# Scores of the prompt from float16 pairs instead of float32r pairs in a two-layer streaming encoder

## The chip, the cores and the metric

The kernel runs on one core of a Trainium2 chip. The core has a matrix engine (TensorE, "PE" in the profile, with its weight loads shown as "PEld"), a vector engine (VectorE, DVE), an activation engine (ScalarE, ACT), a general engine (GpSimd, POOL) and a queue engine (SyncE, SP) from which this kernel issues all its DMA transfers. The metric is the device time of one execution in microseconds (us), as the median of several runs.

## The reference

Two attention layers follow each other, for a prompt of 2048 tokens and, beside it, a sample of 64 new tokens with a cache. Of each layer the shape is this:

```python
def gated_attention_layer(x_p, x_s, ck, cv, norm_g, w_in, q_g, k_g, w_out, ...):
    qp, kp, vp, gp = project(x_p, norm_g, w_in, q_g, k_g, n_heads, n_kv)
    op = prompt_band_attention(qp, kp, vp, past_chunks, bias_fn, sinks)
    y_p = x_p + (op * jax.nn.silu(gp)) @ w_out
    ...                       # the same for the sample, with the cache before its keys

def project(x, norm_g, w_in, q_g, k_g, n_heads, n_kv):
    p = rms_norm(x, norm_g) @ w_in
    ...                       # split in q, k, v, gate
    q = rms_norm(q.reshape(..., HEAD_DIM), q_g)
    k = rms_norm(k.reshape(..., HEAD_DIM), k_g)

def attend(q, k, v, bias, valid, sinks):
    s = einsum('bqkgd,bskd->bkgqs', qg, k) * (dh ** -0.5) + bias
    ...                       # softmax over the keys, in layer A with a learned sink
    o = einsum('bkgqs,bskd->bqkgd', p, v)
```

The model is 1024 wide and a head has 64 dimensions. Layer A has 16 query heads on 2 key heads and looks at its own chunk of 64 tokens and 2 chunks before it; layer B has 16 query and 16 key heads and looks 8 chunks back. All is in float32.

## The kernel before

**Two parts for one number.** To reach nearly float32 with operands of fewer bits, the kernel writes a factor as a sum of a high and a low part. In the projections of layer A both parts are float32r, in those of layer B float16. For the scores before the change, both parts are float32r in both layers.

**How a score is made.** A head has 64 dimensions and a tile 128 partitions, so the high and the low part of the keys lie one above the other: `KA` and `KB` (one for each of two key heads) have 128 partitions, 64 with the high part and 64 with the low part, and one column for each token. The queries come as two stationary matrices: `q1` holds the high part of the query in both halves, `q2` the low part in the half that meets the high part of the keys, and zeros in the other half. Two matmuls that add up in PSUM then give (q high)(k high + k low) + (q low)(k high). The queries are loaded as weights; the keys are the moving operand.

**Who makes the parts.** A transposed tile of queries or keys lies in PSUM. ACT writes the high part with a scale for each dimension (`qsc` is minus the query's norm weight, `ksc` is 8 times the key's; the signs are turned since the kernel works with the negative score). DVE then computes the scaled value minus the high part (lines L1043, L1082, L1343, L1347). The second copy of the high part of the queries, in the other 64 partitions, is made by a DMA from the tile to itself (L1090 in layer A, L1336 in layer B).

**Layer A** (from L1037 on) goes through 4 groups of 4 query heads and, in each, through 17 tiles: 16 of 128 prompt tokens and the sample of 64. A tile has one group of 8 score matmuls (L1121 for `q1`, L1122 for `q2`, for 4 heads) over up to 256 keys. The queries of a tile are made two tiles ahead of their scores.

**Layer B** (from L1307 on) goes through 8 pairs of heads and, in each, through 8 units of 256 prompt tokens and the sample. A unit has 4 groups of score matmuls, one for each half unit and head (L1392 for `q1`, L1393 for `q2`). A half unit looks at up to 640 keys, which the program takes in two pieces: 384 and 256 keys from the fifth tile on, less before. The 640 scores go through DVE (L1396, adds the bias and takes the minimum), ACT (L1400, the exponential), back through PE (L830, transposes), ACT and DVE again (L805, L806, the two parts of the probabilities) and PE (L1487, the product with the values).

**What sets the order.** PE's order is written out by the program: a "filler" hands out the matmuls of the projections and of the output projections, piece by piece, by a running count of their estimated cost, and the attention steps stand between. On ACT, DVE, POOL and SP a scheduler orders the instructions by its own estimate of time. The filler's counts hold no term for the scores.

**The sample** uses the same code, with `KSA`, `KSB` (float32r) as its keys. In layer A its `q1` and `q2` come from the same buffers as the prompt's; in layer B it has a tile `QS` of its own, whose unused blocks are zeros.

Of the kernel before, what the change touches and what calls it, by code (L numbers as in the profile page):

```python
# [55 lines left out]
def hybrid_encoder_kernel(  # L56
# [68 lines left out]
    qsc = const([P, 2], "qsc")  # L125
    ksc = const([P, 2], "ksc")
    kgr = const([P, 2, 2 * HD], "kgr")
    sink = const([P, 16], "sink")
# [4 lines left out]
    def constants():  # L133
        load(qkg, qk_gain)
        load(sink, sinks.partition_broadcast(P))
        load(tab[:32], t5_table)
        held["oh"] = oh = t("row", [P, VL], 2)
        load(oh[:32, :VL], t5_onehot)
        load(kgr, k_gain_row.partition_broadcast(P))
        nc.vector.tensor_scalar(qsc, qkg[:, 0:2], -1.0, 1.0, op0=ALU.mult, op1=ALU.mult)  # L140
        nc.vector.tensor_scalar(ksc, qkg[:, 2:4], HD ** 0.5, 1.0, op0=ALU.mult, op1=ALU.mult)
        nc.vector.tensor_scalar(nsink, sink, -1.0, 1.0, op0=ALU.mult, op1=ALU.mult)
        nc.vector.tensor_scalar(kgr, kgr, HD ** 0.5, 1.0, op0=ALU.mult, op1=ALU.mult)
# [753 lines left out]
    def layer_a():  # L897
# [131 lines left out]
        def keys(it):  # L1029
# [4 lines left out]
            transpose(tp, it.kv[:n, 0:128])  # L1034
            gk = ksc[:, 0:1]
            if it.unit[0] == NU:
# [5 lines left out]
            for kk, rows in zip(kd, halves):  # L1042
                nc.vector.scalar_tensor_tensor(  # L1043
                    kk[64:128], tp[rows], gk[rows], kk[0:64].bitcast(F32),
                    op0=ALU.mult, op1=ALU.subtract,
                )
# [20 lines left out]
        def queries(it, tp):  # L1067
            n = it.tile[2]
            it.q1 = q1 = t("q1", [P, 4, P], 2, F32R)
            it.q2 = q2 = low_queries().rearrange("p (h s) -> p h s", h=4)  # L1070
            d1 = [q1.rearrange("p (j e) s -> p j e s", e=2)[:, :, hh, :n] for hh in range(2)]
            d2 = [q2.rearrange("p (j e) s -> p j e s", e=2)[0:64, :, hh, :n] for hh in range(2)]
            src = [tp[r].rearrange("p (j s) -> p j s", j=2) for r in halves]
            for hh, rows in enumerate(halves):
                nc.scalar.activation(d1[hh][rows], src[hh], AF.Identity, scale=qsc[rows, 0:1])
            it.todo = []
            it.low = d1, d2, src

        def lows(it):
            d1, d2, src = it.low  # L1080
            for hh, rows in enumerate(halves):
                nc.vector.scalar_tensor_tensor(  # L1082
                    d2[hh], src[hh], qsc[rows, 0:1], d1[hh][rows].bitcast(F32),
                    op0=ALU.mult, op1=ALU.subtract,
                )
            for hh, rows in enumerate(halves):
                if it in items[-3:]:
                    nc.scalar.activation(d1[hh][halves[1 - hh]], src[hh], AF.Identity, scale=qsc[rows, 0:1])
                else:
                    load(d1[hh][halves[1 - hh]].bitcast(F32), d1[hh][rows].bitcast(F32))  # L1090

# [146 lines left out]
    def layer_b():  # L1238
# [69 lines left out]
        def queries(it):  # L1308
            for q in it.todo:
                bg.run(q)  # L1310
            u, T, tiles = it.unit
            gk = ksc[:, 1:2]
            if u == 1:
# [16 lines left out]
            for hh, rows in enumerate(halves):  # L1330
                nc.scalar.activation(q1[hh][rows], qt[hh], AF.Identity, scale=qsc[rows, 1:2])
# [9 lines left out]
            def low(hh, rows):  # L1341
                def fn():
                    nc.vector.scalar_tensor_tensor(  # L1343
                        q2[hh][rows], qt[hh], qsc[rows, 1:2], q1[hh][rows].bitcast(F32),
                        op0=ALU.mult, op1=ALU.subtract,
                    )
                    nc.vector.scalar_tensor_tensor(  # L1347
                        kd[hh][halves[1 - hh]], kt[hh], gk[rows], kd[hh][rows].bitcast(F32),
                        op0=ALU.mult, op1=ALU.subtract,
                    )  # L1350
                    if it in its[-2:]:
                        nc.scalar.activation(
                            q1[hh][halves[1 - hh]], qt[hh], AF.Identity, scale=qsc[rows, 1:2]
                        )
# [455 lines left out]
```

## Time and profile before

| | us |
|---|---|
| median of 3 runs | 2246.05 |
| lowest and highest | 2245.26, 2250.43 |
| the profiled execution | 2247.64 |
| its span, from first to last instruction | 2245.9 |

The profiled execution is 1.6 us above the median of the runs, and 1.7 us of its time lie outside its span. Matmuls are pipelined: a matmul's duration in a row runs from its start to the end of its last result, and the next one begins long before that. What a matmul costs in a stream is therefore the distance from its start to the start of the next one. The layers lie in the span as follows: layer A's attention to about 690 us, beside it the projections of layer A; then the output projection of A and the first projections of B; layer B's attention from about 900 to 2087 us; the rest of the output projection of B to the end.

### The profile page before, as it was taken

How to read it: one execution, taken by the hardware profiler on the slowest of the kernel's cores; microseconds unless marked ns; L12 is line 12 of the kernel's file. 1: busy time of each engine (PE TensorE's matmuls, PEld its weight loads, DVE VectorE, ACT ScalarE, POOL GpSimd, SP SyncE). 2: the span in 40 equal slices, each digit the busy share in tenths (PEclk: the TensorE clock that was granted, in tenths of full speed). 3: DMA queues.
4: the chain of work that ended last, by engine and by line, in shares of the span. 5: the costliest groups of instructions: out<-in, count | busy, mean ns of one | idle time of the engine just before them, and what ended most of it. 6: DMA issues, size and time to landing. Idle time of an engine off the chain costs nothing.

```text
span 2245.9 us, 41785 instructions
## 1 busy us (share of the span) xinstructions
PE 2175.9 (97%) x13931; PEld 1651.6 (74%) x13931; DVE 1566.4 (70%) x4042; ACT 1421.1 (63%) x3610; POOL 860.2 (38%) x1396
## 2 busy tenths in 40 slices
PE   7999999999999999999999999999999999998999
PEld 6878888788889997556666666666666666566888
DVE  6768777677675456877676776877767767577652
ACT  6878878677785333666676665766666667566430
POOL 5645544334354455753333333333333333232000
PEclk9999999999999999999999999999999999999999
DMA  8857547856545677554243342432434434223664
GB/s 273 272 164 221 185 131 224 234 165 192 181 136 176 213 208 238 183 167 132 90 150 113 100 151 85 151 106 87 155 95 124 130 88 125 79 70 105 195 196 126
DMA packets 254072, 348.96 MB, mean 155 GB/s; under 512 B 29776, under 2 KB 191328, under 8 KB 253824
## 3 DMA queue, kind: packets, MB, share of 16 engines
q1 hardware_dynamic: 253856, 346.29, 50.6%
q8 instruction: 110, 1.80, 0.3%
q14 instruction: 106, 0.87, 0.1%
HBM read 257.59 MB, written 73.43 MB: 147 GB/s over the span
## 4 chain that ended last, share of the span: by engine, by line
PE 69%; DVE 11%; DMA 7%; ACT 7%; issue 3%; POOL 2%; SPq 1%; ACTq 0%; DVEq 0%; POOLq 0%
PE pj L668 12%; PE pj L670 11%; PE pj L669 11%; PE sb L830 4%; PE pj L1653 4%; PE pj L1654 4%; PE pj L1655 4%; PE o L1487 4%; PE tp L830 2%; DMA scan<-in_w_in_b_dram 2%; PE sb L1392 2%; PE sb L1393 2%; PE sa L830 2%; DVE p L1396 1%; DVE pl L806 1%
## 5 line engine op out<-in xcount | busy, mean ns | idle before, releaser
L668 PE MATMUL pj<-wh,xx 128*128 128x512 f16 (+2 forms) x1648 | 639.6, 388 | 4.2 <-ACT pb L691 3.1
L670 PE MATMUL pj<-wh,xx 128*128 128x512 f16 (+2 forms) x1648 | 624.2, 379 | 2.5 <-POOL xx L553 2.5
L669 PE MATMUL pj<-wh,xx 128*128 128x512 f16 x1024 | 389.6, 380 | 0.0
L1400 ACT ACTIVATE p<-p,nm 128x640 f32<-128x640 f32 (+5 forms) x264 | 199.5, 756 | 230.8 <-DVE nm L1396 228.3
L1653 PE MATMUL pj<-xx,wh 128*128 128x264 f32 (+1 forms) x1024 | 289.6, 283 | 5.1 <-DVE res L1663 3.6
L1654 PE MATMUL pj<-xx,wh 128*128 128x264 f32 (+1 forms) x1024 | 286.9, 280 | 0.0
L806 DVE SCALAR_TENSOR_TENSOR pl<-sb,ph 128x640 f16<-128x640 f32 (+4 forms) x256 | 189.0, 739 | 101.5 <-ACT ph L805 98.9
L669 PE MATMUL pj<-wl,xx 128*128 128x512 f32 (+1 forms) x624 | 233.7, 374 | 2.6 <-DVE wl L459 2.6
L553 POOL TENSOR_TENSOR xx<-xraw,xx 128x528 fp32r<-128x528 f32 (+4 forms) x144 | 184.4, 1300 | 86.5 <-ACT xx L552 80.1
L830 PE MATMUL sb<-ident,p 128*128 128x128 f32 x1144 | 206.7, 277 | 4.6 <-DVE pl L806 2.7
L1232 POOL TENSOR_TENSOR o<-gt,o 128x256 f32<-128x256 f32 (+1 forms) x132 | 100.0, 758 | 285.6 <-ACT p L1138 92.4
L1396 DVE CUSTOM_DVE_ANT_0 p<-sb,BT 128x640 f32<-128x640 f32 (+5 forms) x272 | 196.2, 721 | 18.3 <-PE sb L1393 12.8
L745 POOL TENSOR_TENSOR sq<-pa 128x256 f32<-128x256 f32 (+2 forms) x187 | 113.1, 605 | 228.1 <-ACT pa L704 140.8
L750 POOL TENSOR_TENSOR f<-f,mhalf 128x4 f32<-128x4 f32 (+2 forms) x187 | 191.8, 1026 | 14.1
L830 PEld LDWEIGHTS sb<-ident,p 128*128 128x128 f32 x1144 | 149.2, 141 | 62.7 <-DVE pl L806 16.4
L805 ACT ACTIVATE ph<-sb 128x640 f16<-128x640 f32 (+4 forms) x256 | 160.4, 627 | 54.9 <-PE sb L830 53.5
L670 PEld LDWEIGHTS <-xx 128*128 128x128 f16 x1024 | 100.5, 98 | 124.8 <-POOL xx L553 3.0
L1138 ACT ACTIVATE p<-p,nm 128x257 f32<-128x257 f32 (+2 forms) x272 | 134.3, 497 | 49.6 <-DVE nm L1132 43.5
L668 PEld LDWEIGHTS <-xx 128*128 128x128 f16 x1024 | 100.3, 98 | 77.5 <-ACT xx L552 1.4
L669 PEld LDWEIGHTS <-xx 128*128 128x128 f16 x1024 | 101.1, 99 | 67.6 <-issue 1.9
L1487 PE MATMUL o<-pl,values 128*128 128x256 f16 (+1 forms) x672 | 149.4, 255 | 0.0
L1487 PEld LDWEIGHTS <-values 128*128 128x128 f16 x1344 | 134.1, 101 | 15.8 <-issue 0.2
(258 smaller groups left out, 5391.7 us busy)
## 6 DMA issues: line engine op xcount, KB each, us to landing
xx<-xsb SPq DMA_DIRECT2D x112, 512.0 KB, 3.8
xx<-xsa SPq DMA_DIRECT2D x88, 512.0 KB, 5.0
xraw<-oga SPq DMA_DIRECT2D x64, 264.0 KB, 3.8
xraw<-ogb SPq DMA_DIRECT2D x64, 264.0 KB, 3.7
xsa<-xx SPq DMA_DIRECT2D x32, 512.0 KB, 4.3
scan<-in_w_in_b_dram SPq DMA_DIRECT2D x64, 256.0 KB, 4.5
wl<-in_w_in_b_dram SPq DMA_DIRECT2D x64, 256.0 KB, 4.2
q<-q SPq DMA_DIRECT2D x250, 64.0 KB, 2.7
```

The source lines that it names most:

```text
L553: nc.gpsimd.tensor_tensor(lo, rv, wide(hi), op=ALU.subtract)
L668: nc.tensor.matmul(ps[:n, :C], xh, wh, start=k == 0, stop=False)
L669: nc.tensor.matmul(ps[:n, :C], xh, wl, start=False, stop=False)
L670: nc.tensor.matmul(ps[:n, :C], xl, wh, start=False, stop=k == KC - 1)
L750: nc.gpsimd.tensor_tensor(fv, fv, mhalf[:n, :H], op=ALU.pow)
L806: b = nc.vector.scalar_tensor_tensor(dst_lo, src, scale, wide(dst_hi), op0=ALU.mult, op1=ALU.subtract)
L830: nc.tensor.transpose(out, in_, ident[:n, :n])
L1396: mi = nc.vector.tensor_tensor_reduce(out=p[r, :nk], in0=S[r, o : o + nk], in1=b, op0=ALU.add, op1=ALU.min, scale=1.0, scalar=3e38, accum_ ...
L1400: ex = nc.scalar.activation(p[:n, :nk], p[:n, :nk], AF.Exp, scale=-1.0, bias=it.nm[:n, c : c + 1], accum_out=it.sm[:n, c : c + 1],)
L1487: nc.tensor.matmul(it.O[:, h * T + q0 : h * T + q1_], vt, p[:, c, q0:q1_], start=start, stop=stop)
L1653: nc.tensor.matmul(ps[:, :OT], wh, oh, start=k == 0, stop=False)
L1654: nc.tensor.matmul(ps[:, :OT], wh, ol, start=False, stop=False)
```

## The change

`KA`, `KB`, `q1` and `q2` of the prompt become float16 in both layers, half as many bytes. The range of float16 is narrow, so the scales are dealt out anew: of the product of the two norm weights of a dimension, times 8, the key gets a power of two (`kf`: the exponent of the product, divided by 8, held between 1 and 32768) and the query the rest (`qf`, held within plus and minus 60000). The product of the two scales stays what it was. The sample keeps float32r and the old scales; in layer A its queries now lie in `QS`, `q1` in the left half of each block and `q2` in the right, and `QS` is set to zero once more before layer B.

```diff
@@ constants()
+        nc.vector.tensor_tensor(qf, qsc, ksc, op=ALU.mult)
+        nc.vector.tensor_scalar(kf.bitcast(I32), qf.bitcast(I32), 0x7F800000, None, op0=ALU.bitwise_and)
+        nc.vector.tensor_scalar(kf, kf, 0.125, 1.0, op0=ALU.mult, op1=ALU.max)
+        nc.vector.tensor_scalar(kf, kf, 2.0 ** 15, 1.0, op0=ALU.min, op1=ALU.mult)
+        inv = t("ms", [P, 8])[:, 0:2]
+        nc.vector.reciprocal(inv, kf)
+        nc.vector.tensor_tensor(qf, qf, inv, op=ALU.mult)
+        nc.vector.tensor_scalar(qf, qf, 60000.0, -60000.0, op0=ALU.min, op1=ALU.max)
...
-    KA = const([P, SEQ], "KA", F32R)
-    KB = const([P, SEQ], "KB", F32R)
+    KA = const([P, SEQ], "KA", F16)
+    KB = const([P, SEQ], "KB", F16)
...
-    Q2 = [const([P, 512], f"q2_{i}", F32R) for i in range(2)]
+    Q2 = [const([P, 512], f"q2_{i}", F16) for i in range(2)]
@@ layer A, keys()
-            gk = ksc[:, 0:1]
+            gk = (kf, ksc)[it.unit[0] == NU][:, 0:1]
@@ layer A, queries() and lows()
-            it.q1 = q1 = t("q1", [P, 4, P], 2, F32R)
-            it.q2 = q2 = low_queries().rearrange("p (h s) -> p h s", h=4)
+            if it.unit[0] == NU:
+                it.q1, it.q2 = q1, q2 = QS[:, :, 0:TS], QS[:, :, TS:P]
+            else:
+                it.q1 = q1 = t("q1", [P, 4, P], 2, F16)
+                it.q2 = q2 = low_queries().rearrange("p (h s) -> p h s", h=4)
+            gq = (qf, qsc)[it.unit[0] == NU]
...
-                    load(d1[hh][halves[1 - hh]].bitcast(F32), d1[hh][rows].bitcast(F32))
+                    load(wide(d1[hh][halves[1 - hh]]), wide(d1[hh][rows]))
@@ layer B, queries()
-                it.q1 = t("q1", [P, 2, UT], 2, F32R)
+                it.q1 = t("q1", [P, 2, UT], 2, F16)
...
-                    load(q1[hh][halves[1 - hh]].bitcast(F32), q1[hh][rows].bitcast(F32))
+                    load(wide(q1[hh][halves[1 - hh]]), wide(q1[hh][rows]))
@@ layer B, pipeline()
+            zero(QS)
```

The lines below the new ones in `constants()` move down by 10, and those below layer A's `queries` by 14 to 16, so that L1392 before is L1408 after. On PE, in one group of scores of layer B (`sb` the scores in PSUM, `KB` the keys, `q` the two query matrices, `pj` a projection on either side), there stands before:

```order
L670 LDWEIGHTS xx_19815
L670 MATMUL pj_20023<-wh_18509,xx_19815 128x512
L1392 MATMUL sb_20052<-KB,q_3946_19793 128x384
L1393 MATMUL sb_20052<-KB,q_1_109 128x384
L1392 MATMUL sb_20052<-KB,q_3946_19793 128x256
L1393 MATMUL sb_20052<-KB,q_1_109 128x256
L668 LDWEIGHTS xx_19817
L668 MATMUL pj_20023<-wh_18770,xx_19817 128x512
```

and in the same place after:

```order
L680 LDWEIGHTS xx_19822
L680 MATMUL pj_20030<-wh_18516,xx_19822 128x512
L1408 LDWEIGHTS q_3943_19800
L1408 MATMUL sb_20059<-KB,q_3943_19800 128x384
L1409 LDWEIGHTS q_1_111
L1409 MATMUL sb_20059<-KB,q_1_111 128x384
L1408 LDWEIGHTS q_3943_19800
L1408 MATMUL sb_20059<-KB,q_3943_19800 128x256
L1409 LDWEIGHTS q_1_111
L1409 MATMUL sb_20059<-KB,q_1_111 128x256
L678 LDWEIGHTS xx_19824
L678 MATMUL pj_20030<-wh_18777,xx_19824 128x512
```

A float32r matmul loads its weights itself; a float16 one has the load as an instruction of its own. The program has 1472 such loads more, one for each score matmul of the prompt, and PE's order is otherwise as it was.

On DVE, in the first 16 us of the program (`wl` low parts of the first weights, `qsc`, `ksc`, `kgr` constants, `G` and `o` sums of squares), there stands before:

```order
L140 TENSOR_SCALAR qsc<-qkg 128x2
L141 TENSOR_SCALAR ksc<-qkg 128x2
L142 TENSOR_SCALAR nsink<-sink 128x16
L459 TENSOR_SCALAR wl_179<-wraw_129,gain,wh_178 128x256
L143 TENSOR_SCALAR kgr<-kgr 128x256
L459 TENSOR_SCALAR wl_187<-wraw_133,gain,wh_186 128x256 x2
L580 TENSOR_TENSOR o_49_232<-res_230 128x256
```

and after:

```order
L144 TENSOR_TENSOR qf<-qsc,ksc 128x2
L145 TENSOR_SCALAR kf<-qf 128x2
L146 TENSOR_SCALAR kf<-kf 128x2
L153 TENSOR_SCALAR kgr<-kgr 128x256
L469 TENSOR_SCALAR wl_197<-wraw_135,gain,wh_196 128x256
L147 TENSOR_SCALAR kf<-kf 128x2
L469 TENSOR_SCALAR wl_197<-wraw_135,gain,wh_196 128x256
L149 RECIPROCAL ms_162<-kf 128x2
L590 TENSOR_TENSOR o_50_242<-res_240 128x256
L150 TENSOR_TENSOR qf<-qf,ms_162 128x2
```

The seven new instructions (the last of them, L151, stands a little further on) lie between the splits of the first weights.

On POOL, where layer A ends (`p` with the sinks of the sample's last two pairs of heads, `o` an output, `G` a gate, `xx` the output projection's activations), there stands before:

```order
L1145 TENSOR_TENSOR G_8988<-pb_8584,sm_8974 128x256
L1130 COPY p_9105<-nsink 64x2
L1232 TENSOR_TENSOR o_1996_9083<-gt_9057,o_1996_9083 128x256
L1130 COPY p_9111<-nsink 64x2
L553 TENSOR_TENSOR xx_8941<-xraw_8930,xx_8941 128x528
```

and after:

```order
L1159 TENSOR_TENSOR G_8994<-pb_8591,sm_8980 128x256
L1144 COPY p_9111<-nsink 64x2
L849 MEMSET QS 128x512
L1246 TENSOR_TENSOR o_1993_9089<-gt_9063,o_1993_9089 128x256
L1144 COPY p_9117<-nsink 64x2
L563 TENSOR_TENSOR xx_8947<-xraw_8936,xx_8947 128x528
```

The memset of `QS` waits for the sample's last score matmuls of layer A, which read it, and the copy of the second pair's sinks stands behind it. Elsewhere the orders of ACT, DVE, POOL and SP differ by swaps of neighbours; on SP, the load of one bias tile (L317, the third of the second head group) moves back behind two other loads in the first 65 us.

More of the change, by code (lines that the diff above doesn't have):

```diff
@@ L1043, in keys @@
                 nc.vector.scalar_tensor_tensor(
-                    kk[64:128], tp[rows], gk[rows], kk[0:64].bitcast(F32),
+                    kk[64:128], tp[rows], gk[rows], wide(kk[0:64]),
                     op0=ALU.mult, op1=ALU.subtract,
@@ L1311, in queries @@
             u, T, tiles = it.unit
-            gk = ksc[:, 1:2]
+            sample = u == NU
+            gk, gq = ((kf, qf), (ksc, qsc))[sample]
+            gk, gq = gk[:, 1:2], gq[:, 1:2]
             if u == 1:
@@ L1343, in fn @@
                     nc.vector.scalar_tensor_tensor(
-                        q2[hh][rows], qt[hh], qsc[rows, 1:2], q1[hh][rows].bitcast(F32),
+                        q2[hh][rows], qt[hh], gq[rows], wide(q1[hh][rows]),
                         op0=ALU.mult, op1=ALU.subtract,
@@ L1347, in fn @@
                     nc.vector.scalar_tensor_tensor(
-                        kd[hh][halves[1 - hh]], kt[hh], gk[rows], kd[hh][rows].bitcast(F32),
+                        kd[hh][halves[1 - hh]], kt[hh], gk[rows], wide(kd[hh][rows]),
                         op0=ALU.mult, op1=ALU.subtract,
@@ L1352, in fn @@
                         nc.scalar.activation(
-                            q1[hh][halves[1 - hh]], qt[hh], AF.Identity, scale=qsc[rows, 1:2]
+                            q1[hh][halves[1 - hh]], qt[hh], AF.Identity, scale=gq[rows]
                         )
```

14 lines of the change are left out of this document (8 added, 6 removed).

## The prediction

> **What bounds the kernel now.** I read the busy shares first, then the chain that ended last, then busy time by stretch (columns: stretch, its length, busy us of PE, PEld, DVE, ACT, POOL, granted clock, DMA share, GB/s), then PE's waits.
>
> ```profile
> PE 2175.9 (97%) x13931; PEld 1651.6 (74%) x13931; DVE 1566.4 (70%) x4042; ACT 1421.1 (63%) x3610; POOL 860.2 (38%) x1396
> PE 69%; DVE 11%; DMA 7%; ACT 7%; issue 3%; POOL 2%; SPq 1%; ACTq 0%; DVEq 0%; POOLq 0%
> 60.00:700.00 640.00, 628.63 (x3618) 534.47 (x3617) 467.45 (x1451) 493.91 (x1376) 308.89 (x541) 1.00 0.62 189
> 900.00:2090.00 1190.00, 1160.43 (x7279) 770.60 (x7278) 879.11 (x2167) 776.82 (x1956) 416.80 (x716) 1.00 0.39 118
> PE tp L830 <- ACT gt L1219: 7.8, 6, 2.6
> ...
> PE pj L668 <- ACT pb L712: 0.2, 1, 0.2
> ```
>
> PE is busy 98% of both stretches that hold scores (628.63 of 640, 1160.43 of 1190); DVE, the next engine in layer B, 74%. The list of PE's waits, of which the first and the last row stand here (time in all, times, longest), has 24 rows with 59 waits and 64 us. So PE is the bound, and PE time saved should mostly come off the end.
>
> **What a score matmul costs now.** By shape, there are these (the other two of each four of a shape have the same count: L1393 and `KB` in layer B, L1122 and `KB` in layer A):
>
> ```profile
> L1392 PE MATMUL sb<-KA,q 128*128 128x384 f32 x96 | 49.1, 512 | 3.0 <-ACT q L1352 2.9
> L1392 PE MATMUL sb<-KA,q 128*128 128x256 f32 x128 | 39.1, 308 | 0.0
> L1392 PE MATMUL sb<-KA,q 128*128 128x128 f32 x16 | 6.6, 410 | 0.0
> L1121 PE MATMUL sa<-KA,q 128*128 128x256 f32 x120 | 29.7, 280 | 0.0
> L1121 PE MATMUL sa<-KA,q 128*128 128x128 f32 x8 | 2.6, 343 | 4.0 <-ACT res L647 4.0
> ```
>
> The durations overlap, so the price is the distance between starts. Two full groups (384 and 256 keys) of layer B in order of time, with the float16 projection around them (start us, duration):
>
> ```profile
> 1304.73 0.38 PE L669 MATMUL pj<-wh,xx 128*128 128x512 f16 x1
> 1304.94 0.38 PE L670 MATMUL pj<-wh,xx 128*128 128x512 f16 x1
> 1304.97 0.52 PE L1392 MATMUL sb<-KB,q 128*128 128x384 f32 x1
> ...
> 1305.98 0.38 PE L669 MATMUL pj<-wh,xx 128*128 128x512 f16 x1
> ...
> 1309.35 0.38 PE L670 MATMUL pj<-wh,xx 128*128 128x512 f16 x1
> ...
> 1310.38 0.38 PE L669 MATMUL pj<-wh,xx 128*128 128x512 f16 x1
> ```
>
> From L670 to the L669 behind the group pass 1.04 and 1.03 us. In it lie two projection matmuls (L670 and the L668 after the group) at 0.215 each (0.21 to 0.22 between neighbours such as L669 and L670 here). That leaves 0.61 and 0.60 us for the four score matmuls, the change between the two number formats included.
>
> What float16 matmuls of these widths cost, this kernel shows in the products with the values (256 and 128 columns); beside them a float32r score of 128:
>
> ```profile
> 1307.98 0.22 PE L1487 MATMUL o<-pl,values 128*128 128x128 f16 x1
> 1308.04 0.28 PE L830 MATMUL sb<-ident,p 128*128 128x128 f32 x1
> 1308.15 0.27 PE L1487 MATMUL o<-pl,values 128*128 128x256 f16 x1
> ...
> 1308.92 0.38 PE L668 MATMUL pj<-wh,xx 128*128 128x512 f16 x1
> 909.58 0.28 PE L1393 MATMUL sb<-KB,q 128*128 128x128 f32 x1
> 909.70 0.39 PE L668 MATMUL pj<-wh,xx 128*128 128x512 f16 x1
> ```
>
> Seven matmuls of 256 columns stand between 1308.15 and 1308.92: 0.11 each. One of 128 takes 0.06 (1307.98 to 1308.04); the float32r one takes 0.12. No float16 matmul of 384 columns is in the trace; the three widths that are there lie on one line (0.06, 0.11, 0.215), and I take the middle of the last two, 0.1625.
>
> **The sum on PE.** Full groups in layer B: float16 gives 2 x 0.1625 + 2 x 0.11 = 0.545 against 0.605, 0.06 less; there are 2 x 96 = 192, so 11.5 us. The starts are read to 0.01, which on a group is 0.02 either way, 4 us on 192: ends 7.5 and 15.5. The 128-column matmuls of layer B (4 x 16 = 64) save 0.06 each, 3.8 us. The 256-column ones outside full groups number 4 x (128 - 96) = 128. Their price before is that of layer A:
>
> ```profile
> 338.17 0.27 PE L1121 MATMUL sa<-KA,q 128*128 128x256 f32 x1
> ...
> 339.11 0.40 PE L663 MATMUL pj<-wh,xx 128*128 128x512 f32 x1
> ...
> 347.17 0.28 PE L1121 MATMUL sa<-KA,q 128*128 128x256 f32 x1
> ```
>
> Eight in 0.94 us, 0.1175 each, so 0.0075 less in float16: 1.0 us for the 128. The 64 short groups also save the change of format, which the full groups' 0.605 contains; at an estimated 0.01 each that is 0.6. Layer B: 16.9 us. Layer A: 4 x 120 / 8 = 60 groups at 8 x 0.0075 = 0.06, 3.6 us; 32 matmuls of 128 columns at 0.06, 1.9 us. There the neighbours are float32r, so the format change is now paid on entering and leaving: 64 groups at 0.015, minus 1.0. Layer A: 4.5 us. Together 21.4 us.
>
> The 1472 added weight loads stand before their matmuls as those of the projections and of the products do, and the prices read there contain them; that excludes a loss from them. With the reading error of the full groups the sum lies between 17 and 25 us; I take 21.
>
> [...]
>
> **The other engines.** ACT and DVE write float16 where they wrote float32r. Rows of equal width, out of PSUM:
>
> ```profile
> L806 DVE SCALAR_TENSOR_TENSOR pl<-sb,ph 128x512 f16<-128x512 f32 x16 | 11.0, 689 | 8.9 <-ACT ph L805 8.9
> L803 DVE TENSOR_TENSOR pl<-sa,ph 128x512 fp32r<-128x512 f32 x124 | 81.1, 681 | 0.5 <-ACT ph L802 0.4
> L805 ACT ACTIVATE ph<-sb 128x512 f16<-128x512 f32 x16 | 9.3, 581 | 0.0
> L802 ACT CAST ph<-sa 128x512 fp32r<-128x512 f32 x124 | 68.0, 587 | 23.2 <-PE sa L830 22.6
> ```
>
> The difference is 8 ns up on DVE and 6 down on ACT. Some 400 such instructions on each make at most 3 us of DVE time, hidden in DVE's idle 26%; without that cover 3 us. I take nothing.
>
> Seven small DVE instructions are new at the start:
>
> ```profile
> 12.35 0.16 DVE L141 TENSOR_SCALAR ksc<-qkg 128x2 f32<-128x2 f32 x1
> 12.42 0.16 DVE L142 TENSOR_SCALAR nsink<-sink 128x16 f32<-128x16 f32 x1
> 20.36 1.09 DVE L580 TENSOR_TENSOR G<-res 128x256 f32<-128x256 f32 x1 [1.15 <-ACT res L575]
> ```
>
> Starts are 0.07 apart in a stream and one lasts 0.16: 0.5 to 1.1 us for seven. Queued behind are splits of the first weights, for which PE waits; DVE then stands idle for 1.15 us before 20.36, where the delay ends. Cost nothing; uncovered 1.1 us. The same end holds for the third bias tile on SP, whose readers are scores of the second head group: nothing.
>
> The memset of `QS` on POOL and the copies on SP:
>
> ```profile
> L839 POOL MEMSET QS<- 128x512 f32 x1 | 0.5, 529 | 0.1
> 671.20 0.74 POOL L1232 TENSOR_TENSOR o<-gt,o 128x256 f32<-128x256 f32 x1 [0.65 <-DVE o L1231]
> 337.23 1.29 SPq L1090 DMA_DIRECT2D q<-q  x2
> DMA to landing us min/median/max: 2.0/3.0/6.5
> q<-q SPq DMA_DIRECT2D x6, 32.0 KB, 3.7
> ```
>
> The memset (0.53 us) comes between the sample's two sink copies; POOL is idle for 0.65 us there, before the output at 671.20. Behind it wait the output and the second copy, and for that ACT's exponential; without the cover 0.5 us, once. The memsets of `q2` are half as wide. The copies of the queries have half the bytes in as many rows and issues, so SP's time stays.
>
> **What passes to the end.** A wait of PE ended by work that the scores themselves feed moves along with them; one ended by something else swallows what was saved ahead of it. If each of the 59 waits swallowed one group's 0.06, 3.6 us would be lost. I take 2, and 19 of 21 pass. The profiled execution's 2247.64 (span 2245.9 and 1.7 around it) becomes 2228.6; it lies 1.6 above the median of the runs, so I forecast 2227.
>
> **Rivals.** *Most is swallowed.* Only the 69% of the chain that is PE passes, or less, since DVE, ACT and DMA hold 25% of it: 15 us at 69%, 7 to 14 below that, some 2236. For it speak the many changes of engine in the chain; against it, that the idle time of PE in layer B is 30 us of 1190 and DVE has a quarter free.
>
> *Nothing to measure.* The same, with under a third passing, or the loads of float16 queries not hidden: within 6.7 us, 0.3% of the time, which is about what a measurement can tell from no change. Some 2243. Against it speak the float16 products, which run at 0.11 with a load before each.
>
> *Slower, by the query copies.* In layer A the copy of a prompt tile goes from rows of 512 bytes to rows of 256. It is issued at 337.23, lands after 3.0 (median), and is read at 347.17: about 6 us to spare with the second issue counted. The nearest rows of 256 bytes are the sample's six copies, 3.7 us. To eat 19 us and make 7 more, the 60 groups would each have to wait 0.43, so copies would have to land 9 to 10 us after their issue; the longest before is 6.5. At 9.5 us for all (0.45 each, 27 us on the forecast), 2254. [...]
>
> *It doesn't do what it says.* The separate loads of `q` in PE's order exclude that.
>
> **How the numbers follow.** Forecast (14 to 25 us less, 2221 to 2232) 0.68; mostly swallowed 0.12; more than 25 us, because groups elsewhere gain more than the two shown, 0.06; within 0.3% 0.08; slower 0.06. Faster by over 0.3% is the first three, 0.86. The range leaves out slower, no change and the outer parts of the two cases beside the forecast: 2219 to 2238.
>
> **What would show it.** Right: the full group's distance from L670 to the second projection matmul falls from 1.04 to about 0.98; score matmuls of 256 columns start 0.11 apart; ACT and DVE rows of the queries keep their durations; PE's waits stay near 64 us. Wrong: waits of PE for `q<-q` in layer A, waits in layer B grown by more than 5 us, or score matmuls in float16 with the same distances as now.

## The result, and the profile after

The changed kernel takes 2236.9 us (median of 13 executions, 2230.8 to 2242.5), the kernel before 2247.4 beside it. The ratio is 0.9952, with a 95% interval of 0.9938 to 0.9965: 10.8 us faster, 8 to 14. Forecast were 2227 and a range of 2219 to 2238. The time lies inside the range, but at its slow end: near the 2236 of the rival "most is swallowed", not among the 2221 to 2232 of the forecast's own case. One execution of the kernel before, beside the first experiments, took 4457.8 us, twice as long as the others, and is left out of every comparison.

The profiled execution of the changed kernel is its slowest, 2242.53 us (span 2240.8). Its first two parts to read are again the busy shares and the chain that ended last:

```profile
PE 2162.1 (96%) x13931; PEld 1580.2 (71%) x13931; DVE 1567.7 (70%) x4049; ACT 1419.6 (63%) x3610; POOL 858.4 (38%) x1397
PE 64%; DVE 13%; ACT 9%; DMA 6%; issue 5%; POOL 3%; SPq 1%; ACTq 0%; DVEq 0%; POOLq 0%
```

PE has the same 13931 matmuls and is still the bound, but the chain holds 64% of PE where it held 69%; DVE rose from 11% to 13% and ACT from 7% to 9%. Some of the saved PE time has turned into waiting for those two.

Here is PE in order of time (start us, duration) around a full group of layer B:

```profile
1300.65 0.38 PE L680 MATMUL pj<-wh,xx 128*128 128x512 f16 x1
1300.86 0.33 PE L1408 MATMUL sb<-KB,q 128*128 128x384 f16 x1
1301.02 0.33 PE L1409 MATMUL sb<-KB,q 128*128 128x384 f16 x1
1301.19 0.27 PE L1408 MATMUL sb<-KB,q 128*128 128x256 f16 x1
1301.30 0.27 PE L1409 MATMUL sb<-KB,q 128*128 128x256 f16 x1
1301.40 0.38 PE L678 MATMUL pj<-wh,xx 128*128 128x512 f16 x1
1301.62 0.38 PE L679 MATMUL pj<-wh,xx 128*128 128x512 f16 x1
```

From L680 to the second projection matmul behind the group pass 0.97 us. Before it was 1.04 and 1.03, and 0.98 was forecast. The starts of the 256-column matmuls are 0.11 apart, as forecast, and the 384-column ones 0.16 to 0.17, where the middle of two neighbours gave 0.1625.

Both kernels issue their matmuls in the same order, so each distance can be compared with the one before. Between matmuls 6000 and 11000 (1024 to 1839 us before, 1022 to 1829 after; 130 of the 192 full groups) the distances from the matmul ahead of a group of scores to the second one behind it are 12.0 us shorter in all. Over the whole of layer B the same count gives 16.0; 16.9 was forecast. So the price of the scores was right. But PE gets through that stretch only 7.4 us sooner. Most of the missing 4.6 stands in the waits of PE in that stretch (us in all, times, longest), first of the kernel before and then of the changed one:

```profile
PE tp L830 <- DVE scl L202: 2.7, 4, 0.8
PE tp L830 <- ACT gt L1219: 2.7, 3, 1.0
PE sb L830 <- DVE pl L806: 2.4, 9, 0.5
PE pj L668 <- ACT pb L712: 0.2, 1, 0.2
```

```profile
PE sb L840 <- DVE pl L816: 4.1, 13, 0.9
PE tp L840 <- DVE scl L212: 3.9, 4, 1.1
PE tp L840 <- ACT gt L1233: 2.4, 4, 0.8
PE sb L840 <- DVE nm L1412: 1.5, 4, 0.4
PE tp L211 <- DVE KB L1363: 0.2, 1, 0.2
```

8.0 us became 12.1: waits ahead of transposes (L840), until DVE has made the low part of the turned exponentials of the step before (`pl`), or until it has copied the scales and given up the PSUM tile (`scl`), or until ACT has scaled the gates (`gt`), or, new in this list, until DVE has found the minimum of the scores (`nm`). The second trace of the kernel before, that of the first experiment, has 8.7 us there. PE arrives there sooner and waits for what did not become faster. A changed order of the other engines is not the reason: in this stretch the orders of DVE's and of ACT's work differ between the two kernels in one place only (at about 1121 us), that of POOL's nowhere. Nor does either trace have half clock in it.

The busy time by stretch (columns as in the prediction) shows a second thing, the granted clock:

```profile
900.00:2090.00 1190.00, 1152.51 (x7323) 722.28 (x7322) 882.18 (x2172) 779.52 (x1962) 414.18 (x712) 0.99 0.38 115
437.00:457.00 20.00, 16.62 (x74) 12.57 (x73) 9.39 (x28) 10.52 (x31) 5.80 (x12) 0.83 0.85 228
871.00:891.00 20.00, 14.68 (x64) 6.93 (x63) 10.88 (x21) 6.63 (x17) 11.71 (x13) 0.83 0.95 346
1899.00:1919.00 20.00, 16.24 (x82) 8.68 (x81) 9.71 (x31) 7.47 (x22) 3.46 (x9) 0.83 0.16 51
```

In three stretches of 20 us PE is idle for 3.4 to 5.3 us and the clock is 0.83. In the clock records this is half clock for 6.8 us each time, beginning 2.1 to 2.5 us after PE has gone idle. The kernel before has such stretches too, at the same places in the program. Within the span its records give 13.8 us lost in all (27.6 us at half clock) in the profiled execution, those of the changed kernel 24.4. The changed kernel also has more gaps of that size: behind its first matmul PE stands idle for 1.9 us or more 14 times, in the kernel before 8 times (and 8 times in its second trace).

### The profile page after: what moved, and what is told of

The parts are those of the page before. It is cut to its first block, busy times and chain, and to the rows that moved or that the text cites. A ratio compares the mean times of both kernels' runs of the same rounds, so it can differ in the third digit from the quotient of the medians.

```text
span 2240.8 us, 41683 instructions
## 1 busy us (share of the span) xinstructions
PE 2162.1 (96%) x13931; PEld 1580.2 (71%) x13931; DVE 1567.7 (70%) x4049; ACT 1419.6 (63%) x3610; POOL 858.4 (38%) x1397
## 2 busy tenths in 40 slices
DMA packets 254072, 340.77 MB, mean 152 GB/s; under 512 B 45648, under 2 KB 191328, under 8 KB 253824
## 4 chain that ended last, share of the span: by engine, by line
PE 64%; DVE 13%; ACT 9%; DMA 6%; issue 5%; POOL 3%; SPq 1%; ACTq 0%; DVEq 0%; POOLq 0%
PE pj L678 11%; PE pj L680 11%; PE pj L679 11%; PE pj L1670 4%; PE pj L1672 4%; PE pj L1671 4%; PE sb L840 3%; PE o L1503 3%; PE tp L840 2%; DVE p L1412 2%; DMA scan<-in_w_in_b_dram 2%; PE sa L840 2%; ACT p L1416 2%; DVE pl L816 2%; PE sb L1408 1%
## 5 line engine op out<-in xcount | busy, mean ns | idle before, releaser
L680 PE MATMUL pj<-wh,xx 128*128 128x512 f16 (+2 forms) x1648 | 626.1, 380 | 2.5 <-POOL xx L563 2.5
L840 PE MATMUL sb<-ident,p 128*128 128x128 f32 x1144 | 207.6, 278 | 9.0 <-DVE pl L816 5.7
L840 PEld LDWEIGHTS sb<-ident,p 128*128 128x128 f32 x1144 | 149.7, 142 | 68.5 <-DVE pl L816 20.7
L680 PEld LDWEIGHTS <-xx 128*128 128x128 f16 x1024 | 100.7, 98 | 125.3 <-POOL xx L563 3.0
```

The costliest lines, as they stand in the source:

```text
L680: nc.tensor.matmul(ps[:n, :C], xl, wh, start=False, stop=k == KC - 1)
L840: nc.tensor.transpose(out, in_, ident[:n, :n])
```

## The experiments

Two theories were put against each other. Theory 1: what the scores save is swallowed at waits for DVE and ACT in layer B. Theory 2: the stretches at half clock behind PE's idle gaps ate the missing part. Behind them stand the prediction's rivals: the query copies of layer A, and the seven instructions at the start. The runs were made on several chips, so times are compared through the ratio to the kernel before on the same chip.

**The kernel before against itself.** No edit.

> The kernel before itself, to see how its executions scatter and what clock each had. Theory 1 (the saved PE time is swallowed at waits for DVE and ACT) says nothing of the scatter. Theory 2 (stretches at half clock after PE's idle gaps, which come and go from execution to execution, ate part of the gain): time and mean granted clock go together, about 2.3 us for 0.001 of clock as between the changed kernel's 13 executions, and the kernel before has the higher clock, near 0.994, against 0.989 to 0.994 of the changed one. If theory 2 is wrong, executions of the same clock differ as much as executions of different clocks.

Measured: 2249.6 us, ratio 1.0008 (0.9997 to 1.0020), no difference, to 0.2%. Over its 12 executions and 34 of the same kernel beside it the mean clock is 0.9927, not the 0.994 expected; the changed kernel's 13 have 0.9917. The 12 alone have 0.9919 and the 34 have 0.9929, so two sets of one kernel can lie as far apart. For the changed kernel time and clock go together:

| mean clock | executions | us |
|---|---|---|
| 0.989 | 1 | 2242.5 |
| 0.990 | 3 | 2238.4 to 2240.7 |
| 0.991 | 2 | 2237.1, 2238.2 |
| 0.992 | 2 | 2232.2, 2236.9 |
| 0.993 | 3 | 2230.8 to 2234.1 |
| 0.994 | 2 | 2231.1, 2231.7 |

That is 2.2 us for 0.001, which is 0.001 of the time itself. The kernel before follows its clock less closely (1.7 us for 0.001, with executions of one clock up to 11 us apart). The difference of the mean clocks, 0.0010, is worth an estimated 2.2 us by the changed kernel's slope. That is a part of what is missing, not all.

**Each layer alone.** The float16 keys and queries with their factors in one layer only; the other layer has float32r tiles as before the change:

```diff
 # layer B only, against the changed kernel
-    KA = const([P, SEQ], "KA", F16)
-    KB = const([P, SEQ], "KB", F16)
+    KA, KB = (t(x, [P, SEQ], 1, F32R) for x in ("KA", "KB"))
...
-            gk = (kf, ksc)[it.unit[0] == NU][:, 0:1]
+            gk = ksc[:, 0:1]
...
+            if it is its[0]:
+                new["K"] = [t(x, [P, SEQ], 1, F16) for x in ("KA", "KB")]
```

In layer A only it is the other way round: float16 tiles and the factors `kf`, `qf` up to the end of layer A, and new float32r tiles with `ksc`, `qsc` from the first queries of layer B.

> float16 scores in layer B only; layer A's keys and queries stay float32r. By the groups in the two traces PE saves some 15.5 us here. Theory 1: only about two thirds of it passes, 9 to 10 us less than before (ratio 0.9957). Theory 2: 13 to 15 us less at equal clock, with executions scattered over 5 us either way by the clock.

> float16 scores in layer A only (the factors' seven DVE instructions at the start included). By the groups PE saves 4.6 us here. Theory 1: half is swallowed, and the start takes 1 us, so 1 to 2 us less than before. Theory 2: 3.6 us less at equal clock. Rival, the query copies with 256-byte rows land late: no gain or a loss, with longer waits of PE for q<-q in the trace.

Layer B alone: 2242.28 us, ratio 0.9973 (0.9960 to 0.9986), 6.1 us. Layer A alone: 2242.25, ratio 0.9985 (0.9971 to 0.9999), 3.4 us. Together 9.5 against 10.8 for the whole change, so the parts add within their intervals. Layer A gave 3.4 of the 4.5 that PE was to save there, in an interval from 0.2 to 6.5 that holds both theories' numbers. Layer B gave 6.1 of 16.9: the loss is mostly in layer B, and it is larger than either theory alone had it. The two kernels' mean clocks, 0.9916 and 0.9915, are below that of the kernel before, as theory 2 has it.

The rival of the query copies falls here. Layer A alone is not slower, and the copies land sooner than before. The group of copies in the table of DMA issues (count, KB each, median us from issue to landing), of the kernel before and of the changed one:

```profile
q<-q SPq DMA_DIRECT2D x250, 64.0 KB, 2.7
```

```profile
q<-q SPq DMA_DIRECT2D x250, 32.0 KB, 2.4
```

Half the bytes in as many rows, and the median falls by 0.3 us. These 250 are the copies of both layers. Only those of layer A, 124 of them, go from rows of 512 bytes to rows of 256; with six of the sample's, their time to landing in the kernel before was 2.0, 3.0 and 6.5 us (least, median, most), and is now:

```profile
DMA to landing us min/median/max: 1.9/2.8/6.2
```

The profile counts 45648 packets under 512 bytes in the whole kernel, where it counted 29776. The copies of layer A with the shorter rows did not land later for it, but a little sooner: 2.8 us against 3.0 in the median. PE's waits for `q<-q` in layer A, which the prediction had named as a sign of being wrong, came to 3.1 us before and 6.6 after; but the second trace of the kernel before has 6.4, so this is no effect of the change.

**Idle gaps filled with work.** Transposes of the identity into the PSUM tile that the work behind overwrites, ahead of four known gaps:

```diff
+    def warm(ps, n):
+        for j in range(n):
+            c = j % 4 * P
+            nc.tensor.transpose(ps[:, c : c + P], ident, ident)
...
                     S = psum_a("sa", 512, 4)
+                    if h == 0 and it in (items[0], items[40]):
+                        warm(S, 22)
...
             S = psum_b("sb", 1024, 2)
+            if it is its[-1] and i == 0 and h == 0:
+                warm(S, 22)
...
+        if o + OT == TOK:
+            warm(ps, 38)
```

> The changed kernel with 104 transposes of the identity that nobody reads, put on PE into four of its idle gaps (22 each ahead of the first scores of layer A, of the 41st tile of layer A and of the last unit of layer B, 38 ahead of the last block's token scales), each written into the PSUM tile that the work behind overwrites. Theory 2: the stretches at half clock behind these gaps (3.4 us at 48, 6.8 at 444, 6.8 at 878, 3.4 at 2066 in the changed kernel's trace, 10 us lost at most) go, and the time falls by 5 to 10 us against the changed kernel, to about 2229 (ratio to before 0.992). Theory 1, or a clock that does not follow PE's idle gaps: the same time as the changed kernel, or up to 2 us more where the dummies outlast a gap (ratio 0.995 to 0.996).

Measured: 2241.82 us, ratio 0.9970 (0.9960 to 0.9981): slower than the changed kernel's 0.9952, although the mean clock rose from 0.9917 to 0.9946. By that the clock would not matter. But the waits of PE between 880 and 910 us (us in all, times, longest) show what happened, against those of the changed kernel at the same place in the program:

```profile
PE tp L845 <- DVE pa L778: 6.7, 2, 4.9
```

```profile
PE o L621 <- DVE row L1627: 4.8, 1, 4.8
PE tp L840 <- DVE pa L773: 0.8, 1, 0.8
```

Only PE's order is written out by hand here; that of the other engines is planned when the kernel is built. The 38 transposes ahead of the token scales changed the planned order of DVE's work behind 870 us: the norm scaling `pa` (L778) came later, and PE waited 6.7 us for it in place of 0.8 (its wait for `row`, 1.7 us here, lies ahead of this window). So the run tested two things at once, and it decides nothing. The next has only the other three places, behind which the planned order of DVE's work is the changed kernel's but for the first 100 us and one place in layer A.

```diff
-        if o + OT == TOK:
-            warm(ps, 38)
```

> The changed kernel with 66 transposes of the identity that nobody reads, 22 each ahead of the first scores of layer A, of the 41st tile of layer A and of the last unit of layer B; none ahead of the token scales, where the 38 of the run before changed the order of DVE's work. Theory 2 (half-clock stretches behind PE's idle gaps cost what is missing): the stretches at 48, 444 and 2066 us go, which is 6.8 us at most, and the time falls by 4 to 7 us against the changed kernel (ratio to before 0.992 to 0.993). If the clock is not it, the time stays (0.995).

Measured: 2232.03 us, ratio 0.9932 (0.9917 to 0.9946), mean clock 0.9943. Against the changed kernel's 0.9952 (0.9938 to 0.9965) that is 4.5 us better, with intervals that still touch. By the medians, work that nobody needs made the kernel faster; since the intervals touch, it is not quite shown. The stretch of the 41st tile, with its 22 transposes in it, is now this (compare 16.62 of 20 and a clock of 0.83 in the changed kernel):

```profile
423.00:443.00 20.00, 19.90 (x119) 16.50 (x119) 12.35 (x37) 12.66 (x37) 7.00 (x14) 1.00 0.76 218
```

Full clock, and no gap. This speaks for theory 2, for some 4 us of it.

**The low halves of layer B's projection weights left out.** The 64 instructions of DVE are not issued, and PE multiplies with the high half in their place, once in the changed kernel and once in the kernel before:

```diff
+                        if g:
+                            w.l = wh
+                            continue
                         nc.vector.scalar_tensor_tensor(
                             wl[:, j, :], rv[:, j, :], s, wide(wh[:, j, :]),
```

> The changed kernel without the 64 DVE instructions that make the low halves of layer B's projection weights (0.7 us each, 45 us of DVE in all); PE runs the same matmuls with the high half in their place, so the low part of those weights is left out of the result. Theory 1 (what the scores save in layer B is partly swallowed at waits that DVE ends): together with the same cut in the kernel before, the distance between the two grows from 11 us to 15 to 17, and in the stretch of layer B in which the trace shows 6.8 us of 13.1 passing (from PE's matmul 6000 to 11000), 11 to 13 pass. Theory 2 alone: the distance stays at 11, the stretch at 7. The kernel itself: 4 to 10 us less than the changed one by theory 1, the same by theory 2.

> The same cut (no low halves of layer B's projection weights from DVE, PE's matmuls kept with the high half) in the kernel before. By both theories little changes, since PE waits little for DVE there: 0 to 3 us less than before (ratio 0.9985 to 1). If it gains as much as the changed kernel does, DVE's relief says nothing of the change, and theory 1 falls.

Measured: 2236.37 (ratio 0.9941, 0.9923 to 0.9960) and 2247.25 (0.9997, 0.9985 to 1.0009). The medians are 10.9 us apart, where theory 1 in this form asked for 15 to 17 and theory 2 for 11; 41 us less work on DVE (busy 1527.1 where it was 1567.7) moved neither kernel measurably. The changed kernel gets through the stretch from matmul 6000 to 11000 in 9.4 us less than the kernel before, both with the cut; that lies between the 11 to 13 of theory 1 and the 7 of theory 2. The waits of PE in that stretch of the changed kernel with the cut are these:

```profile
PE tp L843 <- DVE scl L212: 3.8, 4, 1.1
PE sb L843 <- DVE pl L819: 3.1, 10, 0.4
PE tp L843 <- ACT gt L1236: 2.8, 4, 1.0
PE sb L843 <- DVE nm L1415: 1.9, 4, 0.5
PE tp L211 <- DVE KB L1366: 0.2, 1, 0.2
```

11.8 us, about as without the cut. Against theory 1 in this form, then: less work on DVE did not shorten PE's waits for it. But the cut did more than take work away. It also changed the planned order of ACT's and DVE's work in layer B, in some 40 places on ACT, so what the relief alone would do is not shown. My reading is that the waits' lengths come from the chain itself: a DVE or ACT instruction that can only start when PE has ended something, and whose result PE needs next.

**Two things put elsewhere.** The seven instructions for the factors go behind the first projections, and the scales of the output weights from the second and third tile of the last head pair to its sixth and eighth:

```diff
-        nc.vector.tensor_tensor(qf, qsc, ksc, op=ALU.mult)
...
+                held["first"] = held["evac"]
+                factors()
...
-        elif u == 0:
-            (output_top, output_across)[e]()
-        elif at == 2:
+        elif at == 0:
+            output_top()
+        elif at == 5:
+            output_across()
+        elif at == 7:
             output_scales()
```

> The changed kernel with two things put elsewhere: the seven DVE instructions for the factors behind the first projections, and the scales of the output weights from the second tile of the last head pair to its sixth (transposes) and eighth (broadcast). By the prediction's step the seven cost nothing, so their place changes nothing; by the trace of the changed kernel PE waited 1.0 us for DVE's weight splits behind them, which should go. The other move should take away PE's wait of 3.8 us at 1903 us and the stretch at half clock behind it (3.4 us lost), if no other wait takes its place. Together up to 8 us less than the changed kernel (ratio to before 0.992), or nothing where new waits arise.

Measured: 2229.25 us, ratio 0.9912 (0.9897 to 0.9927), some 9 us better than the changed kernel, with intervals apart. About half of it can be seen at the second move. Around 1900 us, where the changed kernel had 16.24 us of PE in 20 at a clock of 0.83, stands now:

```profile
1899.00:1919.00 20.00, 20.00 (x124) 12.16 (x123) 14.07 (x36) 12.08 (x36) 6.58 (x12) 1.00 0.36 101
```

The list of PE's waits has no row any more that answers to this one of the changed kernel, at 1903 us:

```profile
PE tp L196 <- DVE KB L1363: 3.8, 1, 3.8
```

Along the common order of the matmuls the lead over the changed kernel's profiled execution grows by 6.7 us at that place: the wait of 3.8 us and most of the 3.4 lost behind it to half clock. Some of it goes again: two new waits, 0.7 us for `scrow` and 0.9 for `scl`, stand where the scales are made now, and over the 110 us from there on 4.6 us are left. The rest of the 9 is not tied to a place; the five executions ran at a mean clock of 0.9938 against 0.9917. The kernel before has the same wait, so this is no part of the change's own effect.

At the start, the waits of PE in the first 30 us, of the kernel before, the changed one and this one:

```profile
PE o L668 <- ACT wh L456: 6.4, 1, 6.4
PE pj L669 <- DVE wl L459: 2.6, 1, 2.6
PE o L669 <- DVE wl L459: 0.6, 1, 0.6
```

```profile
PE o L678 <- ACT wh L466: 5.9, 1, 5.9
PE pj L679 <- DVE wl L469: 2.5, 1, 2.5
PE o L679 <- DVE wl L469: 1.2, 2, 0.6
```

```profile
PE o L682 <- ACT wh L470: 6.4, 1, 6.4
PE pj L683 <- DVE wl L473: 3.1, 1, 3.1
```

In the changed kernel PE waits 0.6 us longer at the first low weights (1.2 for 0.6). The sums are 9.6, 9.6 and 9.5: the place of the seven instructions changes nothing, as the prediction's step had it.

**Both, in the changed kernel and in the kernel before.** The 66 transposes and the moves together; this measures the change once more, between kernels in which four long gaps are filled or gone:

```diff
# the kernel before: the transposes and the moved scales
# the changed kernel: the transposes, the moved scales, the moved factors
```

> The kernel before with the 66 transposes of the fifth experiment and with the scales of the output weights moved as in the eighth (it has no factors to move). Together with the run behind it this measures the change between kernels in which the two largest idle gaps and their stretches at half clock are gone. Theory 2: the mean clock rises to about 0.995, and the time falls by 6 to 10 us against before (ratio 0.996).

> The changed kernel with the 66 transposes, the moved factors and the moved scales together. If the gains add, 4.6 us of the transposes and 7 of the moves: about 2225 (ratio to before 0.990). Against the run ahead of it: if the half-clock stretches and the start ate part of the change's gain, the distance is 14 to 16 us; if it was all swallowed in layer B, 11 or 12.

Measured: 2237.93 (ratio 0.9980, 0.9969 to 0.9991, mean clock 0.9952) and 2222.66 (ratio 0.9913, 0.9894 to 0.9932, mean clock 0.9958). The kernel before gained 4.5 us, less than the 6 to 10 expected. The two gains in the changed kernel do not add: 0.9913 here, 0.9912 with the moves alone, so on top of the moves the transposes brought nothing that can be measured. The medians are 15.3 us apart, with a 95% interval of 12.0 to 19.6 from resampling the executions. Theory 2 asked for 14 to 16. Between these two the change is worth 15, between the kernels as they are 10.8, though the intervals overlap by 2 us. The clock explains most of the step: here the changed kernel has the higher mean clock, by 0.0006, there the lower one, by 0.0010. At 2.2 us for 0.001 an estimated 14.0 and 13.0 us are left at equal clock. The waits of PE from matmul 6000 to 11000, first of the kernel before with both:

```profile
PE tp L837 <- DVE scl L207: 2.9, 4, 1.0
PE sb L837 <- DVE pl L813: 1.8, 7, 0.5
PE pj L675 <- ACT pb L719: 1.5, 3, 0.9
PE tp L837 <- ACT gt L1228: 1.0, 1, 1.0
PE o L837 <- POOL o L1475: 0.9, 1, 0.9
```

```profile
PE sb L849 <- DVE pl L825: 3.7, 12, 0.7
PE tp L849 <- DVE scl L219: 3.4, 4, 1.1
PE tp L849 <- ACT gt L1245: 2.6, 4, 1.0
PE sb L849 <- DVE nm L1426: 1.5, 4, 0.4
PE sb L1422 <- issue: 0.3, 1, 0.3
PE tp L218 <- DVE KB L1375: 0.2, 1, 0.2
```

8.1 us became 11.7. So the swallowing in layer B is there as well, at about the size it had (3.6 us in this stretch, 4.1 between the kernels as they are); what these two have lost are stretches at half clock (six and four in their traces, with mean clocks of 0.995 and 0.997, where the kernel before has seven at 0.994 and the changed one twelve at 0.989).

**The cut on top of both.**

```diff
+                        if g:
+                            w.l = wh
+                            continue
```

> The kernel before with the transposes and the moved scales, and without DVE's low halves of layer B's projection weights (the high half is used in their place, so the low part of those weights is left out of the result). PE hardly waits for DVE in this kernel: the same time as with the transposes and the moved scales alone, ratio to before 0.998, at most 2 us lower.

> The changed kernel with the transposes, the moved factors and scales, and without the same low halves. If what the groups save on PE (some 22 us by the two traces) is lost only to the half-clock stretches and to waits that DVE's weight splits cause, the distance to the run ahead of it is 18 to 20 us. If the splits only changed which wait takes the saved time, it stays at 15 or 16, as without this cut.

Measured: 2245.38 (ratio 0.9997, 0.9986 to 1.0008) and 2227.73 (0.9914, 0.9896 to 0.9932). The distance of the medians is 17.7 us (15.7 to 21.3 by resampling), below the 18 to 20 of the one case, above the 15 or 16 of the other, and within the interval of the pair without the cut. It grew because the kernel before lost by the cut: 0.9997 against 0.9980. The changed one stayed at 0.9914 against 0.9913. So the cut saves the changed kernel nothing here either. But PE's waits in the stretch from matmul 6000 to 11000 grew by it in both kernels, from 8.1 to 14.2 us and from 11.7 to 17.8, most of all those for `pl`: the changed order of ACT and DVE cost what less work may have gained. That the splits play no part in the swallowing is therefore not shown.

## Why the prediction was right, and where it was wrong

**What bounds the kernel, right.** PE, before and after, busy for 97% and 96% of the span; taking 41 us of work off DVE moved neither kernel measurably.

**The price of the score matmuls, right.** Full groups fell by the 0.06 us forecast, and the groups of layer B together by 16.0 us against 16.9. In layer A an eight-matmul group of 256 columns went from 0.935 us to 0.803, and the float32r matmul behind it from 0.231 to 0.317: 0.05 less in all, against the 0.06 forecast. Of the change between the two formats, which the sum took at an estimated 0.015 us for such a group, this shows 0.017 (0.803 and 0.086 more behind it, less 8 x 0.109); the 0.01 taken for a short group of layer B was an estimate that was not measured by itself.

**What is hidden, right.** The seven instructions at the start: 9.6 us of waits in the first 30 with or without them. The query copies cost nothing that a run showed, and the rows of ACT and DVE that write the queries kept their durations (layer A: 469 and 468 ns on ACT, 482 and 483 on DVE). The rival "slower, by the query copies" is excluded by layer A alone (0.9985) and by its copies' 2.8 us.

**What passes to the end, wrong in size.** "If each of the 59 waits swallowed one group's 0.06, 3.6 us would be lost. I take 2, and 19 of 21 pass." The mechanism was named, but not its size. In the stretch measured, waits grew by 4.1 us where 12.0 were saved, twice the 2 taken for the whole kernel. The 0.06 for each wait was the fault. The four waits for `scl` grew by 0.3 us each, and where PE had arrived just in time before, new waits came up: the rows ahead of transposes (`scl`, `gt`, `pl`, `nm`) went from 16 occurrences to 25. That a wait swallows all that PE has saved since the step whose result it waits for is my reading of this, not something a run isolated. From the first score of layer B to the last, PE's waits went from 27.2 us to 36.4 (the second trace of the kernel before has 28.7), and in the pair with fewer gaps from 23.8 to 30.4. The prediction had called more than 5 us of growth there a sign of being wrong, and waits near 64 us in all a sign of being right: they are 73.4. With 7 to 9 us swallowed, 21 become 12 to 14, about what the two pairs give at equal clock (13.0 and 14.0).

**A term that the sum did not have.** The stretches at half clock. The granted clock stood in the rows that were read (1.00 in both stretches quoted), and the sum took it as given. The 13 executions of the changed kernel ran at 0.9917 against 0.9927: an estimated 2.2 us. Filling three gaps brought 4.5 by the medians, and the change is worth 15.3 where gaps are gone against 10.8 where they are not, and 3.5 of that difference are the clock by the same estimate. So some 2 to 4 us of the missing 8 are here.

Of 21 us saved on PE, then, about 7 to 9 are swallowed in layer B and 2 or more go with the clock, which leaves 10 to 12; 10.8 were measured. The split between the two rests on single traces and on intervals that overlap. A part of the clock's share has a cause that can be seen: the changed kernel's trace has 14 idle gaps of 1.9 us or more where there had been 8 (four of the six more in layer A), and half clock followed 11 of the 14. How much is this, and how much is chance in where the gaps fall, stays open, since there is one trace of the changed kernel, of its slowest execution. That the saved time goes into waits for the DVE and ACT chains is seen in the traces of two pairs; what would shorten these waits was not found.

**The rival "most is swallowed".** Its 2236 is what came out, at a chance of 0.12. That the time lies in the stated range all the same is luck: the range reached 2238 because it took in the inner part of this rival, while the forecast's own term, 19 of 21 passing, missed by 8 us. Against the rival the prediction set that DVE has a quarter of its time free. That was the wrong argument: DVE is busy 70% of the span before and after, and PE's waits for it grew all the same. The chain's 25% on DVE, ACT and DMA spoke for it (the chain's share of PE fell from 69% to 64%), and it should have had more weight; that the share which passes is the chain's 69% or less was not tested.

## What to carry to other kernels

When the busiest engine gets faster in a tightly alternating pipeline, do not let through all that it saves because the others have idle time: a wait for a result that is still being made can swallow the time saved though the other engine, as DVE here, is idle for 30% of the span (PE's waits in layer B went from 27.2 us to 36.4). Count the waits that recur in every step, and those where the engine now arrives just in time. And look at the granted clock behind the longest idle gaps: moving a single wait of 3.8 us out of the way brought 6.7 us at its place, of which 4.6 were left 110 us later, where the change of number format in 1472 matmuls brought 10.8. The fastest kernels of the study are the changed one with the scales of the output weights moved, with or without the 66 transposes (ratios 0.9912 and 0.9913 to the kernel before).

## What was not expected of the hardware

- The granted clock fell to half (0.5 in the clock records) for 3.4 or 6.8 us, in the changed kernel's trace from 2.0 to 3.4 us after PE had gone idle. There 11 of the 14 gaps of 1.9 us or more have such a stretch (a gap of 1.9 at 220 us has one, one of 2.4 at 95 us has none). In the traces of the kernel before and of the changed one the records all begin on one grid of 3.413 us, which lies elsewhere in each of the two. In both, from 24 us on, wherever PE stood idle for more than 2.0 us inside one cell of that grid (5 cells before, 11 after), half clock followed from the cell's end; so where a gap fell decided, beside its length. Ahead of matmul 12441 PE is idle for 2.90 us in both: before, the grid parts the gap into 1.17 and 1.73 us, and the clock stayed at 1.00; after, it lies inside one cell, and half clock followed. One such stretch in 2240 us costs an estimated 1.7 or 3.4 us, half of its length. The 13 executions of the changed kernel have mean clocks from 0.989 (2242.5 us) to 0.994 (2231.1 and 2231.7), 2.2 us for 0.001.
- Work that nobody reads kept the clock up: 22 transposes in a gap of 2.8 us kept it at 1.00 where it had been 0.83 over 20 us.
- Copies in SBUF of 256-byte rows landed after 2.8 us where those of 512-byte rows, twice the bytes, took 3.0 (medians of 130, in layer A, the sample's six among them).
- A float16 group between float32r neighbours cost a little more than its own matmuls: 0.803 us from the first of eight of 256 columns to the float32r matmul behind them, and another 0.086 on that one, against 8 x 0.109 in a stream of float16, 0.017 more in all.
